# Up projection of a one-layer encoder: low halves of raw weight units from an accumulating DMA into buffers of their own, and thirteen pairs through seven products

## The chip, the core and the metric

The kernel runs on one core of one Trainium2 chip. The metric is the device time of one execution in microseconds (us). Three runs of the kernel before gave 1048.84, 1049.99 and 1050.54 us; their median, 1049.99 us, is the time that the change is measured against.

The engines are named as in the profile: PE is TensorE's matrix multiply and PEld its weight load, DVE is VectorE, ACT is ScalarE, POOL is GpSimd, SP is SyncE, whose queue issues most of the DMAs. All data is float32; fp32r is the rounded form of it that PE takes as an operand here.

## What is computed

One layer of an encoder: three token mixers with gated merging, cross-attention into a memory, and a gated MLP with a short causal convolution, over 512 tokens of 1024 channels. The change touches the MLP's first product alone:

```python
def conv_ffn(h, w_up, conv_w, conv_b, w_down):
    u = causal_dwconv(h @ w_up, conv_w) + conv_b      # w_up: 1024 x 5632
    a, b = jnp.split(u, 2, axis=-1)
    return (jax.nn.silu(a) * b) @ w_down              # w_down: 2816 x 1024
...
x = x + conv_ffn(rmsnorm(x, norm_ffn[l]), w_up[l], ffn_conv[l], ffn_conv_b[l], w_down[l])
```

## The kernel before

**Products in split form.** A float32 matrix is used as a high half (its fp32r rounding, made by an ACT copy) and a low half (the rest, made by a DVE subtraction of the high half). A product is then three passes on PE: high weight by high data, high weight by low data, low weight by high data. Weights come in units of 128x1024 float32 (512 KB). `load_unit` issues the load of a unit from the SP queue into one of three buffers `wraw`; `split_unit` (L182, L183) makes `whi` on ACT and `wlo` on DVE, each in one of two buffers (WB = 3, 2, 2).

**The up stage.** `h @ w_up` has 44 units. They are worked in 22 pairs m = 0..21: unit 2m gives channel block m of `a`, unit 2m+1 block m of `b`. `gated(m)` then does the convolution (ACT L1081, four DVE steps on L1083), the silu (ACT L1085) and the product `hid` (DVE L1087).

- A *plain* pair runs `up_product` twice. A unit is 24 matmuls of 512 columns: 16 with `whi` (L203, L204) and 8 with `wlo` (L206).
- A *seven* pair (m in SEVEN, `seven_products`) regards the two units as a 2x2 block matrix a11, a12, a21, a22 over halves of 512 channels and the tokens as two halves of 256, and needs seven half-size products in place of eight. Each (`half_product`) is 12 matmuls of 256 columns: 8 with a high half (L1021, L1024, L1025), 4 with a low half (L1027). It multiplies raw parts (a11, a12, a22) and sums of parts. DVE makes four sums (L1045, L1046, L1050, L1051, in `s12` and `s34`), ACT and DVE split both sum tiles (L1031, L1032: `sh`, `sl`), a1 whole and the half a22 (`whi`, `wlo`, also L1031, L1032). Five DVE steps of 256 columns (L1068 to L1073) put the products together.

SEVEN holds nine pairs: 7, 8, 9, 11, 13, 15, 16, 18, 20. The token sums that they multiply by (`token_forms`) are made behind pair 4 (FORMS).

**What sets the order.** The program is written pair after pair; a scheduler with a timeline of its own then places the instructions of each engine, and pools with a fixed number of buffers add waits: a new tile waits until all readers of the old one are done. Behind pair 18 come the splits of the first ten `hid` (`split_hidden`), behind the up stage those and the sums of the other twelve (`form_pair`), which go into `room` slots: the freed quads first, then eight tiles of pool `extra`. The pool `extra` is opened behind pair 4, where the pool `late` (x, spilled to DRAM by then) is closed. The down stage follows.

Of the kernel before, what the change touches and what calls it, by code (L numbers as in the profile page):

```python
# [78 lines left out]
def build(nc, tc, ctx, x_t, mem_t, w, cols_d, const_d, unit_d, out_t, dbg=None):  # L79
# [910 lines left out]
    def token_forms():  # L990


        pairs = []
        for name in ("14", "23"):
            pairs.append([hquad(f"t{name}{z}", F32R).rearrange("p a b -> p (a b)").rearrange("p (f k n) -> p f k n", f=2, k=4)
                          for z in "hl"])
        for k in range(4):
            e, o = values[k], values[k + 4]
            f = uwork(f"tf{k}")

            def two(t):
                return t.rearrange("p (f n) -> p f n", f=2)

            V.tensor_tensor(e[:, L], e[:, R], e[:, L], ALU.subtract)
            V.tensor_tensor(two(f), two(e), o[:, None, R].to_broadcast([P, 2, T // 2]), ALU.add)
            V.tensor_tensor(e[:, R], f[:, L], o[:, L], ALU.subtract)
# [6 lines left out]
    def half_product(ps, unit, x, behind=None):


        (wh, wl), (xh, xl) = unit, x
        with ExitStack() as order:
            if behind is not None:
                order.enter_context(tc.issue_after(behind.ins))
            new = behind is None  # L1020
            first = PE.matmul(ps, wh[:, block(0)], xh[:, 0], start=new, stop=False, skip_group_check=not new)  # L1021
            for i in range(4):
                if i:
                    PE.matmul(ps, wh[:, block(i)], xh[:, i], start=False, stop=False, skip_group_check=not new)  # L1024
                PE.matmul(ps, wh[:, block(i)], xl[:, i], start=False, stop=False, skip_group_check=not new)  # L1025
            for i in range(4):
                PE.matmul(ps, wl[:, block(i)], xh[:, i], start=False, stop=i == 3, skip_group_check=not new)  # L1027
        return first

    def split_blocks(src, hi, lo):  # L1030
        S.activation(hi, src, AF.Copy)  # L1031
        V.tensor_tensor(lo, src, hi.bitcast(F32), ALU.subtract)  # L1032
        return hi, lo

    def seven_products(m):


        u = UNITS["up"] + 2 * m
        a1, a2 = load_unit(u), load_unit(u + 1)
        a = [(t[:, :T], t[:, T:]) for t in (a1, a2)]  # L1040
        (a11, a12), (a21, a22) = a
        h1, l1 = wp.tile([P, 1024], F32R, tag="whi", name=f"whi{u}", bufs=WB[1]), wp.tile([P, 1024], F32R, tag="wlo", name=f"wlo{u}", bufs=WB[2])
# [1 line left out]
        s12, s34 = wsum(f"s12_{m}"), wsum(f"s34_{m}")
        V.tensor_tensor(s12[:, :T], a21, a22, ALU.subtract)  # L1045
        V.tensor_tensor(s12[:, T:], a11, s12[:, :T], ALU.subtract)  # L1046
        h12, l12 = split_blocks(s12, wsumh(f"sh12_{m}", F32R), wsuml(f"sl12_{m}", F32R))
        h2, l2 = wp.tile([P, 1024], F32R, tag="whi", name=f"whi{u + 1}", bufs=WB[1]), wp.tile([P, 1024], F32R, tag="wlo", name=f"wlo{u + 1}", bufs=WB[2])
# [1 line left out]
        V.tensor_tensor(s34[:, :T], a21, a11, ALU.subtract)  # L1050
        V.tensor_tensor(s34[:, T:], a12, s12[:, T:], ALU.subtract)  # L1051
        h34, l34 = split_blocks(s34, wsumh(f"sh34_{m}", F32R), wsuml(f"sl34_{m}", F32R))
        (b1h, b1l), (b2h, b2l) = halves
        px = dense_ps(f"px{m}")
        py = misc_ps(f"py{m}")
        pz = gdn_ps(f"pz{m}")
        first = half_product(px[:, L], (h1[:, :T], l1[:, :T]), (b1h[:, :, L], b1l[:, :, L]))
        half_product(px[:, R], (h12[:, :T], l12[:, :T]), t_forms[1], first)
        v = uwork(f"v{m}")
        S.activation(v, px, AF.Copy)  # L1060
        first_y = half_product(py[:, L], (h2[:, :T], l2[:, :T]), t_forms[4])
        half_product(pz[:, L], (h12[:, T:], l12[:, T:]), t_forms[2])
        half_product(px[:, L], (h1[:, T:], l1[:, T:]), (b2h[:, :, L], b2l[:, :, L]), first)
# [323 lines left out]
```

## Time and profile before

| | |
|---|---|
| median of three runs | 1049.99 us |
| the profiled execution, its own time | 1050.53 us |
| its span in the trace | 1048.8 us |
| up stage (first up matmul to first down matmul) | 692.38 to 929.11 us |
| PE busy, whole span | 1035.8 us, 99% |
| DVE, ACT, POOL busy, whole span | 756.6, 566.8, 28.7 us |
| granted TensorE clock | 1.00 |

Matmuls are pipelined: a row of 512 columns lasts 0.39 us, but the next one starts about 0.23 us behind it. The pace of PE is read from start to start, and so is that of DVE and ACT, whose rows overlap the next by some tenths of a microsecond or less. A busy share of PE near 1 says that it had an operand all the time.

### The profile page before, as it was taken

Reading aid. Unit: us, or ns where it says so; the run is one execution under the profiler, and the core shown is the slowest. Engines: PE = TensorE matmul, PEld = TensorE weight load, DVE = VectorE, ACT = ScalarE, POOL = GpSimd, SP = SyncE. Lnnn points to the kernel's source line nnn. Section 1 sums busy time; section 2 is a strip of 40 time slices with the busy share of each in tenths; the row PEclk is TensorE's granted clock in tenths of the full one; section 3 lists DMA queues with packets and bytes.
Section 4 is the critical chain, followed back from the end, with each engine's and each line's share of the span. In section 5 each row is a group of like instructions: output and inputs, shape, how many; then the busy total and the mean of one; then the engine's idle time right before and its main releaser. Section 6 shows DMA issues by size and latency. Waiting matters only on the chain.

```text
span 1048.8 us, 14151 instructions
## 1 busy us (share of the span) xinstructions
PE 1035.8 (99%) x5385; PEld 871.1 (83%) x5385; DVE 756.6 (72%) x1252; ACT 566.8 (54%) x936; POOL 28.7 (3%) x82
## 2 busy tenths in 40 slices
PE   9999999999999999999999999999999999999998
PEld 7787888778888888788888888778899999989997
DVE  5787668788455443446657757679898998899873
ACT  6376757646342644654545657655555645655331
POOL 0000000101010000000000000000000000000000
PEclk9999999999999999999999999999999999999999
DMA  6222121211211111222433333142322323233441
GB/s 234 88 93 101 64 78 61 71 61 62 80 61 61 61 41 61 81 81 90 164 108 121 123 105 115 41 161 83 118 100 93 107 96 109 81 105 117 146 156 61
DMA packets 29443, 100.61 MB, mean 96 GB/s; under 512 B 3392, under 2 KB 3648, under 8 KB 28864
## 3 DMA queue, kind: packets, MB, share of 16 engines
q1 hardware_dynamic: 29088, 99.45, 28.1%
q8 instruction: 42, 0.69, 0.3%
q10 hardware_dynamic: 288, 0.27, 0.1%
q14 instruction: 25, 0.20, 0.1%
HBM read 95.51 MB, written 4.19 MB: 95 GB/s over the span
## 4 chain that ended last, share of the span: by engine, by line
PE 94%; DVE 2%; ACT 1%; issue 1%; DMA 1%; SPq 0%; POOL 0%; ACTq 0%; DVEq 0%; POOLq 0%
PE dn L1186 8%; PE up L206 5%; PE up L204 4%; PE up L203 4%; PE g L203 4%; PE g L204 4%; PE g L206 4%; PE gk L374 2%; PE px L1027 2%; PE px L1025 2%; PE dz L1186 2%; PE dx L1186 2%; PE f L203 1%; PE s L206 1%; PE s L204 1%; PE f L206 1%
## 5 line engine op out<-in xcount | busy, mean ns | idle before, releaser
L182 ACT ACTIVATE whi<-wraw 128x1024 fp32r<-128x1024 f32 x133 | 140.7, 1058 | 169.3 <-PE g L204 38.7
L183 DVE TENSOR_TENSOR wlo<-wraw,whi 128x1024 fp32r<-128x1024 f32 x133 | 162.1, 1219 | 44.4 <-ACT whi L182 19.6
L203 PE MATMUL g<-hh,whi 128*128 128x512 f32 x192 | 77.5, 404 | 1.6 <-DVE gate L390 1.6
L204 PE MATMUL g<-hl,whi 128*128 128x512 f32 x192 | 75.7, 394 | 0.0
L204 PE MATMUL up<-xnl,whi 128*128 128x512 f32 x144 | 56.8, 394 | 0.0
L203 PE MATMUL up<-xnh,whi 128*128 128x512 f32 x144 | 56.8, 394 | 0.0
L206 PE MATMUL g<-hh,wlo 128*128 128x512 f32 x192 | 51.5, 401 | 0.0
L1186 PE MATMUL dn<-room,whi 128*128 128x256 f32 (+1 forms) x176 | 49.6, 333 | 0.0
L203 PEld LDWEIGHTS g<-hh,whi 128*128 128x128 f32 x192 | 36.1, 188 | 10.9 <-DVE gate L390 1.4
L206 PEld LDWEIGHTS g<-hh,wlo 128*128 128x128 f32 x192 | 35.8, 188 | 8.3 <-issue 0.5
L204 PEld LDWEIGHTS g<-hl,whi 128*128 128x128 f32 x192 | 36.2, 188 | 7.7
L390 DVE TENSOR_TENSOR gate<-g,r_x 128x512 f32<-128x512 f32 x24 | 16.4, 688 | 30.8 <-PE g L206 30.8
L1083 DVE SCALAR_TENSOR_TENSOR uc<-u,cols,uc 128x511 f32<-128x511 f32 (+1 forms) x52 | 37.0, 745 | 0.9 <-ACT uc L1081 0.9
L206 PE MATMUL up<-xnh,wlo 128*128 128x512 f32 x144 | 36.4, 395 | 0.0
L1186 PE MATMUL dn<-room,wlo 128*128 128x512 f32 (+1 forms) x128 | 34.1, 352 | 0.0
L1186 PEld LDWEIGHTS dn<-room,whi 128*128 128x128 f32 x176 | 29.8, 188 | 3.4
L203 PEld LDWEIGHTS up<-xnh,whi 128*128 128x128 f32 x144 | 27.1, 189 | 6.0
L204 PEld LDWEIGHTS up<-xnl,whi 128*128 128x128 f32 x144 | 27.1, 188 | 6.0
L206 PEld LDWEIGHTS up<-xnh,wlo 128*128 128x128 f32 x144 | 27.0, 188 | 6.2
L1186 PE MATMUL dn<-hidl,whi 128*128 128x512 f32 x80 | 31.6, 395 | 0.0
L1031 ACT ACTIVATE whi<-wraw 128x1024 fp32r<-128x1024 f32 (+1 forms) x18 | 15.2, 845 | 25.6 <-PE up L204 11.9
L1186 PEld LDWEIGHTS dn<-room,wlo 128*128 128x128 f32 x128 | 24.0, 188 | 3.5
(988 smaller groups left out, 2948.3 us busy)
## 6 DMA issues: line engine op xcount, KB each, us to landing
wraw<-w SPq DMA_DIRECT2D x166, 512.0 KB, 3.5
x<-x_t SPq DMA_DIRECT2D x8, 256.0 KB, 6.6
xr<-x_t SPq DMA_DIRECT2D x2, 1024.0 KB, 6.2
x_spill<-xr SPq DMA_DIRECT2D x2, 1024.0 KB, 4.3
x<-x_spill SPq DMA_DIRECT2D x8, 256.0 KB, 4.1
mem_sb<-mem_t SPq DMA_DIRECT2D x4, 256.0 KB, 4.1
wraw<-w SPq DMA_DIRECT2D x2, 256.0 KB, 4.1
inv<-unit ACTq DMA_DIRECT2D x1, 256.0 KB, 3.4
```

The costliest lines, as they stand in the source:

```text
L182: S.activation(hi, raw, AF.Copy)
L183: V.tensor_tensor(lo, raw, hi.bitcast(F32), ALU.subtract)
L203: PE.matmul(ps, hi[:, b], xh, start=first and i == 0, stop=False)
L204: PE.matmul(ps, hi[:, b], xl, start=False, stop=False)
L206: mm = PE.matmul(ps, lo[:, b], xh, start=False, stop=last and i == len(xs) - 1)
L374: pin(PE.matmul(first[h], a[:, c:c + P], b, start=k == 0 and a is hi and b is xh, stop=k == KC - 1 and b is xl))
L390: V.tensor_tensor(dst, ps, r_x, ALU.mult)
L1025: PE.matmul(ps, wh[:, block(i)], xl[:, i], start=False, stop=False, skip_group_check=not new)
L1027: PE.matmul(ps, wl[:, block(i)], xh[:, i], start=False, stop=i == 3, skip_group_check=not new)
L1031: S.activation(hi, src, AF.Copy)
L1083: V.scalar_tensor_tensor(c[:, s:], u[:, :T - s], col("ffn_conv", 3 * j + 2 - s), c[:, s:], ALU.mult, ALU.add)
L1186: mm = PE.matmul(ps[:, z], lhs, rhs, start=first is None, stop=last, skip_group_check=True)
```

## The change

It alters how the low halves of raw weight units are made in the up stage, which pairs run as seven products, and where one pool lies.

- `split_adding` makes a split without DVE: ACT writes minus the high half into a tile `alo`, POOL issues a DMA that adds the unit from DRAM to it (`accum_op=ALU.add`), and ACT makes `whi` as before. `alo` has four buffers of 128x1024 in a pool `ahead`, so two pairs' worth. It serves a1 (512 KB) and a22 (256 KB) of every seven pair, and both units of the plain pairs behind pair 4 (`ADD_PLAIN`; m > FORMS). That is 34 accumulating DMAs. The kernel before has no such DMA.
- SEVEN gains 10, 12, 14, 17, 19 and loses 15: thirteen pairs, with 7 to 14 in one run, 16 to 20 in another. The plain pairs behind pair 4 are 5, 6, 15 and 21.
- `ahead` takes the room of `extra` during the up stage; `extra` opens behind the loop.
- A seven pair puts its outputs together in place, without the tile `w`: again five DVE steps of 256 columns. The splits of the two sum tiles stay on ACT and DVE. Other edits only rename or merge helpers.

```diff
+AHEAD = 4
+ADD_A22 = True
+ADD_PLAIN = (0, 1)
-SEVEN = (7, 8, 9, 11, 13, 15, 16, 18, 20)
+SEVEN = (7, 8, 9, 10, 11, 12, 13, 14, 16, 17, 18, 19, 20)
...
+    ahead = tiles_of("ahead", "a", AHEAD, (1024,))
...
+    def split_adding(u, src, cols, name):
+
+        lo = ahead(f"alo{name}", F32R)[:, :cols.stop - cols.start]
+        hi = wp.tile([P, 1024], F32R, tag="whi", name=f"whi{name}", bufs=WB[1])[:, :cols.stop - cols.start]
+        S.activation(lo, src, AF.Copy, scale=-1.0)
+        G.dma_start(lo, w[u, :, cols], accum_op=ALU.add)
+        S.activation(hi, src, AF.Copy)
+        return hi, lo
...
+        h1, l1 = split_adding(u, a1, slice(0, 2 * T), f"{u}")
+        s1, s2, f12 = sums("12")
+        V.tensor_tensor(s1, a21, a22, ALU.subtract)
+        V.tensor_tensor(s2, a11, s1, ALU.subtract)
+        w5, w6 = f12()
+        if ADD_A22:
+            h2, l2 = split_adding(u + 1, a22, slice(T, 2 * T), f"{u + 1}")
...
-        split_blocks(a1, h1, l1)
...
-        split_blocks(a22, h2[:, :T], l2[:, :T])
...
-        mm3(ps, split_unit(UNITS["up"] + 2 * m + z), [block(k) for k in range(KC)], x, True, True)
+        u = UNITS["up"] + 2 * m + z
+        if z in ADD_PLAIN and m > FORMS:
+            unit = split_adding(u, load_unit(u), slice(0, 2 * T), f"{u}")
+        else:
+            unit = split_unit(u)
+        mm3(ps, unit, [block(k) for k in range(KC)], x, True, True)
...
             late.close()
-            open_pool("extra", ctx, side="right")
+            room = ExitStack()
+            open_pool("ahead", room, side="right")
         for _ in range(SPLITS.get(m, 0)):
             split_hidden()
+    room.close()
+    open_pool("extra", ctx, side="right")
```

The order in which the built program's instructions stand shows three places. A name ends in the number of its allocation. First, ACT in a seven pair, before: pair 11. `whi_7007` and `whi_7019` are the high halves of a1 and a22, `sh_11` those of the sums, `v` and `u` outputs of pair 9.

```order
L1031 ACTIVATE whi_7007<-wraw_7003 128x1024
L1031 ACTIVATE sh_11_7015<-s_11_7011 128x1024
L1070 ACTIVATE u_6911<-px_6821 128x256
L1031 ACTIVATE sh_11_7025<-s_11_7012 128x1024
L1031 ACTIVATE whi_7019<-wraw_7005 128x512
L1081 ACTIVATE uc_6919<-u_6911,cols 128x512
```

After: the same stretch for pair 10. `alo_7077` and `alo_7089` are the negated high halves of pair 11, one pair ahead of the others; POOL's DMA adds to each when it is written.

```order
L294 ACTIVATE whi_6942<-wraw_6937 128x1024
L292 ACTIVATE alo_7077<-wraw_7073 128x1024
L273 ACTIVATE sh_10_6949<-s_10_6946 128x1024
L1120 ACTIVATE uc_6790<-uc_6790 128x512
L294 ACTIVATE whi_6954<-wraw_6939 128x512
L292 ACTIVATE alo_7089<-wraw_7075 128x512
L273 ACTIVATE sh_10_6961<-s_10_6958 128x1024
L333 ACTIVATE u_6918<-px_6829 128x256
```

Two ACT copies per pair came in, each ahead of a sum's high half of the pair before it. Second, DVE in seven pairs 8 and 9, before:

```order
L1032 TENSOR_TENSOR sl_8_6673<-s_8_6668,sh_8_6672 128x1024
L1073 TENSOR_TENSOR u_6641<-px_6551,w_6640 128x256
L1032 TENSOR_TENSOR sl_8_6683<-s_8_6669,sh_8_6682 128x1024
L1045 TENSOR_TENSOR s_9_6803<-wraw_6797 128x512
L1032 TENSOR_TENSOR wlo_6800<-wraw_6795,whi_6799 128x1024
L1083 SCALAR_TENSOR_TENSOR uc_6649<-u_6641,cols,uc_6649 128x511
L1050 TENSOR_TENSOR s_9_6804<-wraw_6797,wraw_6795 128x512
```

After, the same place:

```order
L332 TENSOR_TENSOR u_6646<-px_6557,u_6646 128x256
L331 TENSOR_TENSOR u_6647<-u_6647,v_6584 128x256
L274 TENSOR_TENSOR sl_8_6690<-s_8_6686,sh_8_6689 128x1024
L1118 SCALAR_TENSOR_TENSOR uc_6654<-u_6646,cols,uc_6654 128x511
L314 TENSOR_TENSOR s_9_6822<-wraw_6803,wraw_6801 128x512
L315 TENSOR_TENSOR s_9_6822<-wraw_6801,s_9_6810 128x512
L1118 SCALAR_TENSOR_TENSOR uc_6658<-u_6647,cols,uc_6658 128x511
```

The subtraction `wlo` is gone; sums and splits of sums stay. Third, PE where the first low half of a seven pair is read, before (pair 7; in brackets what a row waits for):

```order
L1024 MATMUL pz_6553<-t23h,sh_7_6537 128x256
L1025 MATMUL pz_6553<-t23l,sh_7_6537 128x256
L1027 MATMUL px_6551<-xnh_5997,wlo_6530 128x256 [waits DVE_49]
L1027 MATMUL px_6551<-xnh_5997,wlo_6530 128x256 x3
L1021 MATMUL px_6551<-t14h,sh_7_6537 128x256
```

After (pair 8):

```order
L266 MATMUL px_6693<-xnh_5997,whi_6670 128x256
L267 MATMUL px_6693<-xnl_5998,whi_6670 128x256
L269 MATMUL px_6693<-xnh_5997,alo_6669 128x256 [waits DMASW6_49]
L269 MATMUL px_6693<-xnh_5997,alo_6669 128x256 x3
L263 MATMUL px_6693<-t14h,sh_8_6677 128x256 [waits Activation_49]
```

The low-half rows now wait for a DMA that POOL issued, where they waited for DVE. POOL has no other instruction behind pair 4. All engines' rows up to pair 4 stand as before.

## Rows read from the trace of the kernel before

**Rows 1.** The page: span and busy time of each engine, and the first line of the chain that ended last, by engine.

```profile
span 1048.8 us, 14151 instructions
...
PE 1035.8 (99%) x5385; PEld 871.1 (83%) x5385; DVE 756.6 (72%) x1252; ACT 566.8 (54%) x936; POOL 28.7 (3%) x82
...
PE 94%; DVE 2%; ACT 1%; issue 1%; DMA 1%; SPq 0%; POOL 0%; ACTq 0%; DVEq 0%; POOLq 0%
```

**Rows 2.** Busy time of each engine in stretches of the up stage and the start of the down stage: from and to, length, busy time of PE, PEld, DVE, ACT and POOL (with counts), granted clock, DMA share (mean of the 16 engines), GB/s.

```profile
768.00:800.00 32.00, 32.00 (x241) 30.64 (x240) 30.34 (x45) 17.27 (x23) 0.00 (x0) 1.00 0.35 118
800.00:840.00 40.00, 40.00 (x259) 36.34 (x258) 35.75 (x55) 22.55 (x30) 0.00 (x0) 1.00 0.31 103
840.00:880.00 40.00, 40.00 (x274) 37.09 (x274) 35.83 (x55) 20.72 (x28) 0.00 (x0) 1.00 0.32 106
880.00:920.00 40.00, 40.00 (x255) 36.22 (x254) 34.88 (x52) 25.25 (x38) 0.00 (x0) 1.00 0.27 93
```

**Rows 3.** What PE and its weight load waited for from 690 us to the end of the span: us in total, times, longest. It is the whole answer for both.

```profile
PE up L204 <- DVE xfl L196: 0.7, 2, 0.5
...
PEld up L204 <- DVE xfl L196: 1.6, 2, 1.0
```

**Rows 4.** PE in order of time (start, us, line, operation, count): the first matmul of the up stage, the first of one plain unit, that unit's low-half rows and the first matmul of the next unit, and the first of the down stage.

```profile
692.38 0.39 PE L203 MATMUL up<-xfh,whi 128*128 128x512 f32 x1
...
716.36 0.39 PE L203 MATMUL up<-xfh,whi 128*128 128x512 f32 x1
...
720.08 2.02 PE L206 MATMUL up<-xfh,wlo 128*128 128x512 f32 x8
721.93 0.40 PE L203 MATMUL up<-xfh,whi 128*128 128x512 f32 x1
...
929.11 0.40 PE L1186 MATMUL dn<-room,whi 128*128 128x512 f32 x1
```

**Rows 5.** The same view in seven pairs: the first matmul of one half product of 12, its low-half rows and the first matmul behind it; and the same of another.

```profile
777.84 0.28 PE L1021 MATMUL py<-t23h,sh 128*128 128x256 f32 x1
...
778.80 0.64 PE L1027 MATMUL py<-t23h,sl 128*128 128x256 f32 x4
779.28 0.28 PE L1021 MATMUL px<-xnh,whi 128*128 128x256 f32 x1
...
781.53 0.28 PE L1021 MATMUL px<-xnh,sh 128*128 128x256 f32 x1
...
782.49 0.64 PE L1027 MATMUL px<-xnh,sl 128*128 128x256 f32 x4
782.97 0.28 PE L1025 MATMUL px<-xnl,whi 128*128 128x256 f32 x1
```

**Rows 6.** DVE in order of time, a stretch without idle time in a seven pair.

```profile
783.47 0.42 DVE L1072 SCALAR_TENSOR_TENSOR u<-py,w 128x256 f32<-128x256 f32 x1
783.80 1.22 DVE L1032 TENSOR_TENSOR sl<-s,sh 128x1024 fp32r<-128x1024 f32 x1
784.93 0.42 DVE L1073 TENSOR_TENSOR u<-px,w 128x256 f32<-128x256 f32 x1
785.27 1.22 DVE L1032 TENSOR_TENSOR sl<-s,sh 128x1024 fp32r<-128x1024 f32 x1
786.40 0.68 DVE L1045 TENSOR_TENSOR s<-wraw 128x512 f32<-128x512 f32 x1
787.00 1.22 DVE L1032 TENSOR_TENSOR wlo<-wraw,whi 128x1024 fp32r<-128x1024 f32 x1
788.14 0.74 DVE L1083 SCALAR_TENSOR_TENSOR uc<-u,cols,uc 128x511 f32<-128x511 f32 x1
788.80 0.69 DVE L1050 TENSOR_TENSOR s<-wraw,wraw 128x512 f32<-128x512 f32 x1
789.40 0.75 DVE L1083 SCALAR_TENSOR_TENSOR uc<-u,cols,uc 128x511 f32<-128x511 f32 x1
```

**Rows 7.** ACT in order of time: a half-size copy, the silu, the `v` copy and the `u` copy of seven pairs, and a stretch without idle time.

```profile
885.11 0.63 ACT L1031 ACTIVATE whi<-wraw 128x512 fp32r<-128x512 f32 x1 [1.43 <-PE up L204]
...
887.87 0.63 ACT L1085 ACTIVATE uc<-uc 128x512 f32<-128x512 f32 x1
889.85 0.60 ACT L1060 ACTIVATE v<-px 128x512 f32<-128x512 f32 x1 [1.34 <-PE px L1027]
...
896.99 0.39 ACT L1070 ACTIVATE u<-px 128x256 f32<-128x256 f32 x1 [2.05 <-PE px L1027]
...
900.57 0.80 ACT L1081 ACTIVATE uc<-u,cols 128x512 f32<-128x512 f32 x1
901.27 1.04 ACT L1031 ACTIVATE sh<-s 128x1024 fp32r<-128x1024 f32 x1
902.22 1.04 ACT L1031 ACTIVATE whi<-wraw 128x1024 fp32r<-128x1024 f32 x1
```

**Rows 8.** The page's DMA queue that carries all loads (packets, MB, time of its packets as a share of the 16 engines' span) and three of its issues (count, KB each, median us from issue to landing).

```profile
q1 hardware_dynamic: 29088, 99.45, 28.1%
...
wraw<-w SPq DMA_DIRECT2D x166, 512.0 KB, 3.5
...
xr<-x_t SPq DMA_DIRECT2D x2, 1024.0 KB, 6.2
x_spill<-xr SPq DMA_DIRECT2D x2, 1024.0 KB, 4.3
```

More of the change, by code (lines that the diff above doesn't have):

```diff
@@ L239, in project_heads, with two, half_product @@
                 yield 2 * g + q, ps
+    LEFT, RIGHT = slice(0, T // 2), slice(T // 2, T)
+    def two(t):
+        return t.rearrange("p (f n) -> p f n", f=2)
+    def half_product(ps, unit, xs, behind=None):
+        wh, wl = unit
+        with ExitStack() as order:
+            if behind is not None:
+                order.enter_context(tc.issue_after(behind.ins))
+            new = behind is None
+            first = PE.matmul(ps, wh[:, block(0)], xs[0][0], start=new, stop=False, skip_group_check=not new)
+            for i, (xh, xl) in enumerate(xs):
+                if i:
+                    PE.matmul(ps, wh[:, block(i)], xh, start=False, stop=False, skip_group_check=not new)
+                PE.matmul(ps, wh[:, block(i)], xl, start=False, stop=False, skip_group_check=not new)
+            for i, (xh, _) in enumerate(xs):
+                PE.matmul(ps, wl[:, block(i)], xh, start=False, stop=i == 3, skip_group_check=not new)
+        return first
@@ new lines, in split_blocks, with halves_of, sums_of_tokens @@
+    def split_blocks(src, hi, lo):
+        S.activation(hi, src, AF.Copy)
+        V.tensor_tensor(lo, src, hi.bitcast(F32), ALU.subtract)
+        return hi, lo
+    def halves_of(xs, h, z):
+        return [(hi[:, z], lo[:, z]) for hi, lo in xs[4 * h:4 * h + 4]]
+    def sums_of_tokens(e, o, f):
+        V.tensor_tensor(e[:, LEFT], e[:, RIGHT], e[:, LEFT], ALU.subtract)
+        V.tensor_tensor(two(f), two(e), o[:, None, RIGHT].to_broadcast([P, 2, T // 2]), ALU.add)
+        V.tensor_tensor(e[:, RIGHT], f[:, LEFT], o[:, LEFT], ALU.subtract)
@@ L996, in token_forms @@
                           for z in "hl"])
+        forms = {1: [], 2: [], 3: [], 4: []}
         for k in range(4):
[L998 to L1006, printed above, removed]
@@ L1007, in token_forms @@
-            for t, (hi, lo) in zip((e, f), pairs):
+            e, f = values[k], uwork(f"tf{k}")
+            sums_of_tokens(e, values[k + 4], f)
+            for t, (hi, lo), (p, q) in zip((e, f), pairs, ((1, 4), (2, 3))):
                 S.activation(hi[:, :, k], two(t), AF.Copy)
                 V.tensor_tensor(lo[:, :, k], two(t), hi[:, :, k].bitcast(F32), ALU.subtract)
-        (h14, l14), (h23, l23) = pairs
-        return {1: (h14[:, 0], l14[:, 0]), 4: (h14[:, 1], l14[:, 1]), 2: (h23[:, 0], l23[:, 0]), 3: (h23[:, 1], l23[:, 1])}
@@ L1013, in half_product @@
[L1013 to L1042, printed above, removed]
-        split_blocks(a1, h1, l1)
[L1044 to L1048, printed above, removed]
-        split_blocks(a22, h2[:, :T], l2[:, :T])
[L1050 to L1063, printed above, removed]
-        half_product(py[:, R], (h34[:, :T], l34[:, :T]), t_forms[3], first_y)
-        half_product(px[:, R], (h34[:, T:], l34[:, T:]), (b2h[:, :, R], b2l[:, :, R]), first)
-        w = uwork(f"w{m}")
-        u0, u1 = uwork(f"u{m}"), uwork(f"u{m + NF}")
-        V.tensor_tensor(w[:, L], pz[:, L], v[:, L], ALU.add)
-        V.tensor_tensor(w[:, R], py[:, R], w[:, L], ALU.add)
-        S.activation(u0[:, L], px[:, L], AF.Copy)
-        V.tensor_tensor(u1[:, R], w[:, R], v[:, R], ALU.add)
-        V.scalar_tensor_tensor(u1[:, L], py[:, L], -1.0, w[:, R], ALU.mult, ALU.add)
-        V.tensor_tensor(u0[:, R], px[:, R], w[:, L], ALU.add)
-        return u0, u1
@@ new lines, in token_forms, with seven_up, sums, split_sums @@
+                for z, i in enumerate((p, q)):
+                    forms[i].append((hi[:, z, k], lo[:, z, k]))
+        return forms
+    def seven_up(m):
+        def sums(which):
+            t = wsum(f"s{which}_{m}")
+            def split_sums():
+                h, l = split_blocks(t, wsumh(f"sh{which}_{m}", F32R), wsuml(f"sl{which}_{m}", F32R))
+                return [(h[:, z], l[:, z]) for z in (slice(0, T), slice(T, 2 * T))]
+            return t[:, :T], t[:, T:], split_sums
+        return seven(UNITS["up"] + 2 * m, str(m), xn, t_forms, sums, lambda: (uwork(f"u{m}"), uwork(f"u{m + NF}")), uwork)
```

75 lines of the change are left out of this document (50 added, 25 removed).

## The prediction

> **What bounds the kernel now.** I read the page first: PE is busy 99% of the span and 94% of the chain that ended last is PE [rows 1]. The second view is the table of stretches: from 768 to 920 us PE is busy in every microsecond, the granted clock is 1.00, DVE is busy for 30.34 of 32 us, then 35 of 40, ACT for about half, POOL not at all [rows 2]. The third is the list of waits: behind 690 us PE and its weight load wait for others 0.7 and 1.6 us in all, at the start of the up stage [rows 3]. So PE is the bound and never starves. There is no stall to remove: the time falls only by work taken from PE, and only while every operand still comes in time. DVE is the engine next to it, and stands between PE and more seven pairs.
>
> **The gain on PE.** A plain unit takes from 716.36 to 721.93, 5.57 us for 24 matmuls [rows 4], a pair 11.14. A half product of 12 takes 1.44 us (777.84 to 779.28, and 781.53 to 782.97) [rows 5], seven of them 10.08. Check against the whole stage: 692.38 to 929.11 is 236.7 us [rows 4]; 13 x 11.14 + 9 x 10.08 = 235.5, and with the 1.2 us that is left, waits of [rows 3], it closes. A pair that changes sides therefore gives 1.06 us of PE; four more seven pairs (13 for 9) give **4.2 us**. The down stage keeps its matmuls.
>
> **DVE.** From start to start in [rows 6] a step of 1024 columns takes 1.13 us (783.80 to 784.93), of 512 0.60 (786.40 to 787.00), the convolution's 0.66 (788.14 to 788.80), of 256 0.34. A seven pair before: three splits of 1024 (3.39), one of 512 and four sums (3.00), five outputs (1.70), four convolution steps (2.64), one product (0.60): 11.33 us, more than PE's 10.08. A plain pair: 2.26 + 2.64 + 0.60 = 5.50. Before, seven pairs were therefore mixed with plain ones. The eight in a row that the change makes (7 to 14) would need 90.6 us of DVE for 80.6 of PE if they were split the old way. The change takes one split of 1024 and one of 512 away: 9.60 us per seven pair, 76.8 for the run, 95% of PE's time; a plain pair behind pair 4 falls to 3.24. Pairs 7 to 21 together: before 9 x 11.33 + 6 x 5.50 = 135, after 13 x 9.60 + 2 x 3.24 = 131. DVE stays under PE, though hardly in the run. Its relief by itself costs and gives nothing, as PE hides it; it is what allows the 4.2.
>
> **ACT.** Each seven pair gains a copy of 1024 (0.95 from start to start, 901.27 to 902.22) and one of 512 (0.63) [rows 7]. Its sum: four of 1024 (3.80), two of 512 (1.26), `v` 0.60, `u` 0.39, two scalings at 0.70, the silu 0.63: 8.1 of 10.08 us, 80%. Hidden by PE; if ACT comes late, the sums' high halves, which stand behind `alo` on it, make PE wait. A waiting `alo` holds up exactly those: it waits for its raw unit and for a free buffer.
>
> **POOL and the accumulating DMA.** POOL's queue holds nothing else in this stage, so each of the 34 issues waits for its own ACT copy alone; the first also for the spill of x, whose two issues precede nearly all of the up stage's loads, and pair 5 is only due 55 us into it (5 x 11.14). What the trace does not show is how long such a DMA takes. From below: a plain load of the same 512 KB lands in 3.5 us. From above: a read of 512 KB and behind it one with twice the bytes, 3.5 + 6.2 = 9.7 us [rows 8]. It must read two operands of 512 KB, so the nearest row is the 1024 KB load, 6.2 us; I take that.
>
> The Trainium skill, "Collectives: The Full Stack", section "The bandwidth ceiling: the fold count and why AG ≠ RS ≠ AR", says that an addition inside the DMA engine costs no cycles of its own but needs two source reads, which halves the rate (62 against 32 GB/s there). By it the accumulating DMA is an estimated twice a plain one; no run here shows it yet, and it lies on the value that the rows gave.
>
> How long may it take? In the built program's order `alo` of pair 13 stands on ACT ahead of `sh` of pair 12, which PE needs at the second product of pair 12. From there to the first use of pair 13's low half PE has 56 matmuls of 256 columns at 0.12 us (1.44 / 12), 6.7 us, and the `sh` copy takes 0.95: at least 7.6 us of lead, if ACT is only just in time. Some seven of the 512 KB DMAs have a lead near that, most others 10.5 us (80 matmuls) or more. The 256 KB ones have 6.4 us or more, for half the bytes. At 6.2 us all land in time. Nothing is then on PE's path.
>
> **DMA engines.** The 99.45 MB of loads take 28.1% of the engines' span [rows 8], 295 us for all 16, so 1.55 us per 512 KB. A seven pair loads two units (3.1 us) and adds 768 KB: at twice the price of a load 4.7 us, together 7.8 of 10.08. The share rises from 0.31-0.35 [rows 2] to about 0.8. The Trainium skill, "DMA: Bandwidth & Descriptors", section "Issuing engines are not separate DMA queues", speaks against the change here: DMAs of every issuing engine share the same 16 engines. By it the raw loads land later than 3.5 us; the share above already counts them together. The three raw buffers bear some of it: held from the `alo` copy to the `whi` copy, one pair at most, two units need 2 x (3.5 + 10.1) = 27 us of 3 x 10.1 = 30.
>
> **Sum.** The profiled execution took 1050.53 us (span 1048.8, 1.7 around it), 0.54 above the median of the runs. 1050.5 - 4.2 = 1046.3 against it; against the median 1050.0, 1045.8. I forecast **1045.8**, 0.4% faster.
>
> **Rivals.**
> 1. *DVE or ACT becomes the bound in the run of seven pairs* and eats the gain. For it: 95% and 80% load, in queues that wait for each other and for PE in turn. Against: from 768 to 800 us, three old seven pairs, DVE reached 95% and PE missed nothing [rows 2]. If DVE gets through only the 89% of its time that it was busy from 800 to 880, the run takes 76.8 / 0.89 = 86.3 in place of 80.6: 5.7 us lost, 1051.5; at 95% (30.34 / 32) 80.9, 0.3 lost. Middle about 1049.
> 2. *The accumulating DMA lands late* (the slower side). Place: PE's first low-half matmul of each product, which holds up all of PE, since its queue goes in order. It decides from 7.6 us on. At the upper bound of 9.7 us seven of the DMAs miss by 2 us: 14 us, 1060, less where ACT ran ahead. The gain is gone at about 8.2 us. A worse form: the DMA engines fill up. 3.1 + 2.33 k reaches 10.08 at k = 3, k being the price of an added byte in plain ones; at k = 4 each seven pair takes 2.3 us more and each plain one 4.4 us, 1093. For it: no row shows such a DMA; POOL makes its descriptors, unlike SP's. Against: k = 2 by the bytes moved.
> 3. *The change does not do what it says*, the pairs give no time: 1050. It needs a half product of 1.59 us, where two in [rows 5] agree on 1.44; unlikely.
>
> **How the numbers follow.** Forecast (PE stays fed, 1044.5 to 1047.5) 0.59; rival 1 0.18 (1046.5 to 1051.5); rival 2 0.20 (two thirds below 1060); rival 3 0.03. What this kernel's measurement can tell from no change is 0.2%, 2.1 us: faster is below 1047.9, slower above 1052.1. Faster: 0.59 + 0.04 of rival 1 = 0.63. Same: 0.14 + 0.03 = 0.17. Slower: 0.20. The range goes from 1044.5 (the sum, less the 1.2 us by which runs lay under the median) to 1055, which takes in rival 1 and the milder part of rival 2; about 0.17 is left out above it, 0.02 below.
>
> **What the profile after would show.** If right: the up stage ends at about 925 us, PE waits in it as little as before, DVE's `wlo` subtractions are gone behind pair 4, accumulating DMAs land in 5 to 7 us, DMA share 0.7 to 0.8, DVE near 95% from pair 7 to 14. If rival 1: PE waits for `sh`, `sl` or `whi` in pairs 8 to 14, with DVE at 100%. If rival 2: PE waits for DMA at the `alo` rows. The prediction is wrong if such a DMA takes over 8 us, or if a wait for the raw units spreads through ACT's queue.

## The result, and the profile after

The changed kernel takes **1044.27 us** (median of four, 1043.75 to 1044.74) against 1050.03 us of the kernel before in the same runs: ratio 0.9947, 95% interval [0.9929, 0.9964]. It is faster, as forecast, and 0.2 us below the low end of the range. The profiled execution took 1044.74 us. Its page, for [rows 1, 8]: span, busy time, the queue of the accumulating DMAs, and the issues (count, KB each, us to landing).

```profile
span 1043.0 us, 14582 instructions
...
PE 1029.4 (99%) x5529; PEld 873.1 (84%) x5529; DVE 748.8 (72%) x1262; ACT 602.8 (58%) x986; POOL 58.1 (6%) x116
...
q1 hardware_dynamic: 29088, 99.45, 28.3%
q0 software_dynamic: 4896, 14.42, 8.4%
...
wraw<-w SPq DMA_DIRECT2D x166, 512.0 KB, 3.5
alo<-w POOLq DMA_DIRECT2D x21, 512.0 KB, 6.4
alo<-w POOLq DMA_DIRECT2D x13, 256.0 KB, 5.8
```

PE is still the bound. The stretches of [rows 2], after:

```profile
768.00:800.00 32.00, 32.00 (x258) 31.37 (x258) 27.02 (x44) 23.32 (x33) 6.03 (x7) 1.00 0.78 177
800.00:840.00 40.00, 40.00 (x339) 40.00 (x338) 36.84 (x61) 30.93 (x43) 6.90 (x8) 1.00 0.76 182
840.00:880.00 40.00, 40.00 (x293) 37.86 (x293) 34.40 (x56) 30.90 (x42) 6.90 (x8) 1.00 0.83 192
880.00:920.00 40.00, 40.00 (x306) 38.50 (x305) 37.70 (x65) 32.69 (x50) 4.31 (x5) 1.00 0.69 160
```

PE is full in all four, the DMA share has risen from about 0.3 to 0.8, ACT from about half to 73 to 82%, and DVE, with more pairs to serve, is busy 84 to 94%. What PE and its weight load waited for behind 690 us is the whole of [rows 3] again, and nothing else:

```profile
PE up L213 <- DVE xfl L205: 0.7, 2, 0.5
```

```profile
PEld up L213 <- DVE xfl L205: 1.6, 2, 1.0
```

The up stage (first `up` matmul to first `dn` matmul) runs from 691.28 to 923.27, 231.99 us in place of 236.73: 4.74 less. The down stage is as long as before. The other 1.1 us between these two traces lie before the up stage, in instructions that the change does not touch. They go back to the first products of the program. PE in order of time there, in the kernel before, and then in a second profile of the changed kernel (a2):

```profile
6.25 2.07 PE L374 MATMUL gk<-hh,ghi 128*128 128x512 f32 x4 [0.68 <-ACT hh L366]
8.12 1.91 PE L374 MATMUL gk<-hh,glo 128*128 128x512 f32 x4
9.83 1.36 PE L374 MATMUL gk<-hl,ghi 128*128 128x512 f32 x4
11.03 1.10 PE L374 MATMUL gk<-hh,ghi 128*128 128x512 f32 x4
```

```profile
6.13 1.20 PE L469 MATMUL gk<-hh,ghi 128*128 128x512 f32 x4 [1.00 <-ACT hh L461]
7.16 1.10 PE L469 MATMUL gk<-hh,glo 128*128 128x512 f32 x4
8.10 1.08 PE L469 MATMUL gk<-hl,ghi 128*128 128x512 f32 x4
9.02 1.10 PE L469 MATMUL gk<-hh,ghi 128*128 128x512 f32 x4
```

Four matmuls go from start to start in 1.87 us in the first and 1.03 in the second. This is TensorE's clock. Each trace holds a record of the granted clock; it begins, at the upper of the two levels (2.4 GHz), at 10.40 us in the first profile and at 4.46 us in the second. Ahead of that point matmuls of 512 columns start 0.43 us apart, behind it 0.23. The pace of 0.43 is that of the lower level (1.2 GHz): in e4, where the record shows that level from 791.3 to 798.2 us, matmuls of 256 columns start 0.21 us apart, and 0.12 outside it.

Such a **late beginning** puts the products behind it back by 1.7 to 2.1 us. Between the profiles before and after it was 1.7 us; 1.1 of them are left at the up stage, since on the way there one wait of PE, for an ACT copy of a weight, was 0.5 us longer after than before (0.8 against 0.3). Is it of the kernel or of the execution? The experiments had to say.

### The profile page after: what moved, and what is told of

Read it like the earlier page. It is cut to its first block, busy times and chain, and to the rows that moved or that the text cites. A ratio compares the mean times of both kernels' runs of the same rounds, so it can differ in the third digit from the quotient of the medians.

```text
span 1043.0 us, 14582 instructions
## 1 busy us (share of the span) xinstructions
PE 1029.4 (99%) x5529; PEld 873.1 (84%) x5529; DVE 748.8 (72%) x1262; ACT 602.8 (58%) x986; POOL 58.1 (6%) x116
## 3 DMA queue, kind: packets, MB, share of 16 engines
q1 hardware_dynamic: 29088, 99.45, 28.3%
q0 software_dynamic: 4896, 14.42, 8.4%
## 4 chain that ended last, share of the span: by engine, by line
PE 94%; DVE 2%; ACT 1%; DMA 1%; issue 1%; SPq 0%; POOL 0%; ACTq 0%; DVEq 0%; POOLq 0%
PE dn L1221 8%; PE g L212 4%; PE g L213 4%; PE g L215 4%; PE up L215 3%; PE up L213 3%; PE up L212 3%; PE px L267 2%; PE px L269 2%; PE gk L469 2%; PE px L266 2%; PE dz L1221 2%; PE dx L1221 2%; PE f L212 1%; PE s L213 1%; PE s L215 1%
## 5 line engine op out<-in xcount | busy, mean ns | idle before, releaser
L186 ACT ACTIVATE whi<-wraw 128x1024 fp32r<-128x1024 f32 x117 | 123.8, 1058 | 150.4 <-PE g L213 38.7
L187 DVE TENSOR_TENSOR wlo<-wraw,whi 128x1024 fp32r<-128x1024 f32 x117 | 142.7, 1220 | 42.7 <-ACT whi L186 21.4
L293 POOL DMA_DIRECT2D alo<-w x34 | 29.5, 866 | 422.2 <-ACT alo L292 419.8
L294 ACT ACTIVATE whi<-wraw 128x1024 fp32r<-128x1024 f32 (+1 forms) x34 | 30.3, 892 | 15.9 <-PE py L267 8.8
L292 ACT ACTIVATE alo<-wraw 128x1024 fp32r<-128x1024 f32 (+1 forms) x34 | 30.2, 887 | 13.1 <-DMA wraw<-w 12.1
L274 DVE TENSOR_TENSOR sl<-s,sh 128x1024 fp32r<-128x1024 f32 x26 | 31.8, 1223 | 5.2 <-ACT sh L273 5.1
L212 PE MATMUL up<-xnh,whi 128*128 128x512 f32 x80 | 31.6, 395 | 0.0
L213 PE MATMUL up<-xnl,whi 128*128 128x512 f32 x80 | 31.6, 395 | 0.0
L273 ACT ACTIVATE sh<-s 128x1024 fp32r<-128x1024 f32 x26 | 27.3, 1051 | 5.6 <-PE px L267 3.2
L1116 ACT ACTIVATE uc<-u,cols 128x512 f32<-128x512 f32 x34 | 26.7, 809 | 4.5 <-DVE u L1191 3.6
```

The source lines that it names most:

```text
L186: S.activation(hi, raw, AF.Copy)
L187: V.tensor_tensor(lo, raw, hi.bitcast(F32), ALU.subtract)
L212: PE.matmul(ps, hi[:, b], xh, start=first and i == 0, stop=False)
L213: PE.matmul(ps, hi[:, b], xl, start=False, stop=False)
L292: S.activation(lo, src, AF.Copy, scale=-1.0)
L293: G.dma_start(lo, w[u, :, cols], accum_op=ALU.add)
```

## The experiments

The theory: four pairs give what a pair gives, nothing else changed, and the late beginning belongs to the execution. Rivals: the adding DMA gives or costs something by itself; DVE had room for more pairs anyway; the changed program itself begins earlier.

**a1 and a2: both kernels unchanged.**

> The kernel before, unchanged, against itself. Question: how much of the 5.6 us between the medians is variation between executions, and does the first stretch of the program (where the profile of after was 1.1 us ahead, in instructions that are the same in both) vary. Theory 1 (the 1.1 us come from one profiled execution and not from the kernel): ratio 1.000 with an interval that may reach 0.1%, the up stage (first up product to first down product) again 236.7 +- 0.1 us, and its beginning anywhere from 691.2 to 692.5 us. Theory 2 (the changed kernel's first stretch is itself faster): the up stage begins at 692.3 to 692.5 us again.

> The changed kernel, unchanged, in more rounds. Theory 1 (four more pairs at 1.14 us each, nothing else): up stage 232.0 us, 4.6 to 4.8 us shorter than that of before, and the time 4.6 us below before, ratio 0.9955 to 0.9957. Theory 2 (something besides the pairs, worth 1 us): ratio 0.9946 again.

a1: 1049.02 us, ratio 0.9998 [0.9989, 1.0007], up stage 237.03, beginning at 691.0: early, as theory 1 has it, though both figures lie 0.2 us outside those of theory 1. a2: 1044.12 us, ratio 0.9949 [0.9936, 0.9961], up stage 232.37; the interval holds the ratios of both theories, and the stage, 4.66 us shorter than a1's, speaks for theory 1. Over all runs, 90 executions of the kernel before fall into 60 from 1048.04 to 1049.74 (median 1048.92) and 30 from 1049.99 to 1051.21 (median 1050.55), though only 0.25 us lie between the groups. Of the first three, on whose median the forecast rested, two were of the upper group, the profiled one among them. The stages differ by 236.9 - 232.2 = 4.7 us in the mean of the two profiles each.

**f0: the changed kernel a third time.**

> The changed kernel a third time. Question: do its executions ever begin late, as 12 of 31 of the kernel before did in one batch (times from 1050.0 up, against 1048.3 to 1049.7 for the others). Theory 1 (a late beginning has nothing to do with the change, nine early ones were chance): with each further execution a chance of about 0.3 to 0.4 of a time of 1045.5 to 1046.5, so one to three of the new ones. Theory 2 (the changed program begins early always): all of them 1043.7 to 1044.8.

1044.33 us, ratio 0.9951 [0.9937, 0.9965], with two of five at 1045.45 and 1045.59. The profiled one is of these, and shows the late beginning in the changed kernel (its clock record begins at 10.72 us):

```profile
6.16 2.08 PE L469 MATMUL gk<-hh,ghi 128*128 128x512 f32 x4 [0.59 <-ACT hh L461]
8.04 1.91 PE L469 MATMUL gk<-hh,glo 128*128 128x512 f32 x4
```

Its up stage is 231.99 us all the same. Theory 1: the late beginning is the execution's. Median of all 14 executions of the changed kernel 1044.24, of all 90 of the kernel before 1049.07.

**e1: the adding DMA without the four pairs.** **e6: eleven pairs.**

```diff
-SEVEN = (7, 8, 9, 10, 11, 12, 13, 14, 16, 17, 18, 19, 20)
+SEVEN = (7, 8, 9, 11, 13, 15, 16, 18, 20)          # e1
+SEVEN = (7, 8, 9, 10, 11, 12, 13, 15, 16, 18, 20)  # e6
```

> The accumulating DMA alone: the changed kernel with the nine pairs of before in seven products. TensorE then has the work of before. Theory 1 (the adding DMA only makes room on VectorE, and by itself is worth nothing): up stage 236.7 us, ratio 1.000 within 0.1%. Theory 2 (VectorE or its share of SBUF held TensorE up somewhere, so the relief is worth time by itself): up stage shorter by over 0.5 us, ratio below 0.9993. Theory 3 (the doubled DMA work costs something that the gain of the pairs hides): ratio above 1.0007.

> Eleven pairs through seven products (7 to 13, 15, 16, 18, 20), the dose between nine and thirteen, everything else as in the changed kernel. Theory 1 (each pair gives the same, no threshold): up stage 234.4 to 234.5 us, half way between 236.7 and 232.2, time 1046.2 to 1046.5 us where the changed kernel has 1044.1. Theory 2 (the gain of the pairs is partly eaten by something that sets in with the long runs): less than half of the gain is missing, 1045 us or under.

e1: 1048.54 us, ratio 0.9993 [0.9985, 1.0002], up stage 236.74, where the kernel before had 236.73 and 237.03. e1 holds every edit of the change but the pairs. Relieving DVE gives nothing by itself, and the adding DMA's extra work costs nothing. e6: 1046.38 us, ratio 0.9974 [0.9965, 0.9984], up stage 234.38, half way. The gain goes by the number of pairs. The size of a pair is read from start to start of the same matmul of two pairs; in the changed kernel, two seven pairs in a row:

```profile
782.50 0.28 PE L263 MATMUL px<-t14h,sh 128*128 128x256 f32 x1
```

```profile
792.48 0.28 PE L263 MATMUL px<-t14h,sh 128*128 128x256 f32 x1
```

9.98 us a seven pair. In e1, over a seven pair and a plain one:

```profile
791.52 0.28 PE L263 MATMUL px<-t14h,sh 128*128 128x256 f32 x1
```

```profile
812.69 0.28 PE L263 MATMUL px<-t14h,sh 128*128 128x256 f32 x1
```

21.17, so a plain pair takes 11.19, and the exchange is worth **1.21 us**. Read by itself, from its first matmul to the first one behind it, a plain pair of e1 takes 11.17; the other 0.02 lie where it borders on a seven pair:

```profile
800.09 0.39 PE L212 MATMUL up<-xnh,whi 128*128 128x512 f32 x1
...
811.26 0.28 PE L263 MATMUL px<-xnh,whi 128*128 128x256 f32 x1
```

By the stages, a pair is worth 1.17 (a1 against a2) to 1.19 us (before against after).

**e2: the thirteen pairs without the adding DMA.** **e5: DVE splits a22 alone again.**

```diff
-ADD_A22 = True
-ADD_PLAIN = (0, 1)
+ADD_A22 = False   # e2 and e5
+ADD_PLAIN = ()    # e2
...
-        h1, l1 = split_adding(u, a1, slice(0, 2 * T), f"{u}")
+        h1, l1 = (wp.tile([P, 1024], F32R, tag=t, name=f"{t}{u}", bufs=b) for t, b in (("whi", WB[1]), ("wlo", WB[2])))   # e2
+        split_blocks(a1, h1, l1)   # e2
```

> The pairs alone: thirteen pairs in seven products, but all low halves split by VectorE as before, no accumulating DMA. Theory 1 (VectorE needs 11.3 us for a pair of which TensorE needs 10.0): in the run of eight pairs VectorE falls behind by 8 x 1.3 = 10 us, less what its buffers hold (one pair at most), so TensorE waits 3 to 10 us there, and up to 6 us more in the run of five; the time is 1047 to 1056 us, the gain of 4.6 us mostly or wholly lost. Theory 2 (VectorE keeps pace from the slack of the plain pairs, and the adding DMA was not needed): TensorE waits under 0.5 us, the time is that of the changed kernel, 1044 to 1046 us.

> The changed kernel with the 256 KB accumulating DMA left out: the low half of the fourth block of each pair is split by VectorE again, the 512 KB ones stay. VectorE then needs 10.2 us for a pair of which TensorE needs 10.0. Theory 1 (VectorE binds where its work per pair is over TensorE's, less one pair of cushion): 8 x 0.2 = 1.6 us behind in the run of eight, all within the cushion, so the time of the changed kernel within 0.5 us, 1044.1 to 1044.6. Theory 2 (no cushion, the excess of 13 pairs is paid in full, with the hand-overs): 2 to 5 us over it, 1046 to 1049.

e2: 1055.40 us, ratio 1.0058 [1.0046, 1.0071]. DVE (the third busy time) has no idle time left, and PE (the first) starves:

```profile
800.00:840.00 40.00, 37.71 (x305) 36.44 (x304) 40.00 (x64) 24.16 (x33) 0.00 (x0) 1.00 0.29 93
840.00:880.00 40.00, 38.75 (x273) 35.84 (x273) 39.50 (x62) 23.20 (x32) 0.00 (x0) 1.00 0.29 94
```

So the pairs need the DMA: without it they cost 6.1 us against the kernel before (1049.32 in that batch), with it, in a2, they save 5.2. e5 missed both expectations: 1055.92 us, ratio 1.0058 [1.0037, 1.0079], as slow as e2, for 0.60 us of DVE work a pair. DVE is not full: busy 36.41 of 40 us from 800 to 840. PE waits, and then DVE's:

```profile
PE px L263 <- ACT sh L273: 4.2, 3, 2.1
PE px L263 <- ACT v L321: 2.2, 3, 1.4
PE px L263 <- ACT whi L294: 1.7, 1, 1.7
PE py L269 <- DVE wlo L274: 1.7, 4, 0.7
```

```profile
DVE uc L1118 <- ACT uc L1116: 11.4, 7, 4.4
DVE sl L274 <- ACT sh L273: 6.1, 5, 1.5
...
DVE s L305 <- DMA wraw<-w: 4.1, 4, 2.0
```

PE waits for ACT, DVE for ACT and for a raw unit: time lost in hand-overs between queues, not in an engine without rest. PE's waits in this list, 9.8 us, are most of the 13.2 by which the up stage is longer than the changed kernel's (245.4 us).

**e4: two buffers for the adding DMA, not four.** **e9: a copy in the place of the addition.**

```diff
-AHEAD = 4
+AHEAD = 2                                       # e4
...
-        G.dma_start(lo, w[u, :, cols], accum_op=ALU.add)
+        G.dma_start(lo, w[u, :, cols])          # e9
```

> The changed kernel with two buffers for the adding DMA, not four: a pair's first buffer is then free only when the product before the last two of the pair ahead has been read. Theory 1 (landing takes 6.4 us after the issue, as in the profile, and the lead decides): the copy (1.1 us), the issue (0.9 us) and the landing need some 8 us, TensorE can cover 2.9 us of two products and 0.9 us of the next one's first matmuls, so it waits some 4 us for the adding DMA in each of the pairs that follow a pair: 40 to 60 us over the changed kernel, 1085 to 1105. Theory 2 (the landing time is mostly queueing behind other transfers and shrinks when fewer are ahead): half of that or less, 1045 to 1065.

> The changed kernel with a plain copy in the place of the accumulating one, on the same queue, of the same bytes (so the low halves hold whole weights, and the subtraction is left out). Theory 1 (accumulating costs the second time): the queue's share of DMA time falls from 8.4% to 4 to 5%, that is from 3.2 to 1.6 us of sixteen engines per 512 KB, landing from 6.0 to 6.4 us to about 3.5 to 4, DMA share between 770 and 920 us from 0.76 to 0.83 down to about 0.5. Theory 2 (it is the price of this queue, not of adding): share and landing as before. The time stays at 1044 us either way, since TensorE waited for none of these transfers.

e4: 1092.42 us, ratio 1.0401 [1.0358, 1.0444], the time of theory 1, though by another sum: PE waits for the adding DMA once in each of the thirteen pairs, but for 2.2 us and not some 4:

```profile
PE px L269 <- DMA alo<-w: 29.2, 13, 3.1
PE up L215 <- DMA alo<-w: 1.9, 3, 1.1
PE py L269 <- DMA alo<-w: 1.8, 3, 0.8
```

That is 33 of some 50 us. Much of the rest is TensorE's clock (the eighth field): the granted clock was 0.87 to 0.96 in the stretches from 768 to 960 us, 1.00 in those of the changed kernel. The trace has 30.7 us there at the lower level; at 0.21 us a matmul in place of 0.12 that is an estimated 13 us at most.

```profile
768.00:800.00 32.00, 24.99 (x168) 23.44 (x167) 18.93 (x29) 15.54 (x21) 4.28 (x5) 0.89 0.53 130
800.00:840.00 40.00, 34.83 (x274) 34.03 (x274) 29.41 (x48) 25.19 (x35) 5.18 (x6) 0.96 0.60 145
```

So "one pair ahead" is what makes the adding DMA free. e9: 1044.75 us in its one execution, with the queue's work and the landings cut:

```profile
q0 software_dynamic: 4896, 14.42, 4.6%
...
alo<-w POOLq DMA_DIRECT2D x21, 512.0 KB, 4.7
alo<-w POOLq DMA_DIRECT2D x13, 256.0 KB, 4.2
```

8.4% of 1043.0 us for 14.42 MB is 3.19 us of the 16 engines per 512 KB; the copy takes 4.6%, 1.74; a load of SP's queue 1.56 (28.3% for 99.45 MB). The addition nearly doubles the work, theory 1; the DMA share from 770 to 920 us falls from 0.77 to 0.56. But the copy lands in 4.7 us, not the 3.5 to 4 expected, still 1.2 us behind a load of SP's: of the 2.9 us by which the adding DMA is later, 1.7 go with the addition and 1.2 with the rest of this path.

**e3 and e7: fifteen pairs. e8: e5 with more room. e10: seventeen. f1, f2, f3, g1: fourteen. e11: thirteen.** Could more be had? e3 and g1 change SEVEN alone (15 and 21 added; 6 added). The others also load a pair's second unit into the idle `wlo` buffers, which makes five raw buffers of three (e8: into `ahead`).

```diff
-        a1, a2 = load_unit(u), load_unit(u + 1)
+        a1 = load_unit(u)
+        a2 = wp.tile([P, 1024], F32, tag="wlo", name=f"wraw{u + 1}", bufs=WB[2])
+        nc.sync.dma_start(a2, w[u + 1])
```

> Fifteen pairs through seven products: pairs 15 and 21 as well, so that all from 7 to 21 are. Theory 1 (a pair is worth 1.1 to 1.2 us wherever VectorE, ScalarE and the adding DMA keep up, and they do): 2.3 us below the changed kernel, 1041.8 us, no new waits of TensorE. Theory 2 (VectorE's slack is used up: it was busy 94% between 880 and 920 us in the changed kernel, and two more pairs put some 10 us of work on it, 146 of 150 us from 770 to 920): TensorE waits for VectorE for 2 to 8 us in the last pairs or at the start of the down stage, and the time is that of the changed kernel or up to 4 us over it.

> Fifteen pairs through seven products, as in e3, with one edit: the second weight unit of each such pair is loaded into the two buffers that held low halves before and stand idle in this stage, so five raw buffers stand in the place of three. No engine's work changes. Theory 1 (what held e3 up is the ring load - sums - buffer free - next load with only three raw buffers, not the sum of VectorE's work): TensorE's waits go, up stage 229.6 to 229.8 us (two more pairs at 1.2 us under the changed kernel's 232.0 to 232.4), time 1041.6 to 1042.2. Theory 2 (VectorE's total work binds, 97% of the stretch): the waits of e3 stay, 1050 us or more.

> The kernel of e5 (fourth block's low half by VectorE, 256 KB adding DMA left out) with one edit: the second unit of each pair is loaded into the buffers of the adding DMA, of which this kernel uses one of two per pair, so raw units have more room. Theory 1 (e5 lost its 11.8 us to the ring of three raw buffers, which that split held longer, while VectorE was under 92% busy): time of the changed kernel again, 1044.0 to 1045.0. Theory 2 (VectorE, at 10.2 us of work against 9.98 of TensorE per pair, binds): TensorE waits stay, 1050 us or more. In between, 1045 to 1050, both share.

> All pairs from 5 to 21 through seven products, seventeen, with the five raw buffers of e7. Theory 1 (each pair is worth 1.2 us as long as nothing waits): 1039.3 to 1040.0 us, up stage 227.2 to 227.5 us. Theory 2 (VectorE, which also forms the token sums and splits of this stage between 735 and 770 us and was busy 88% there, falls behind at the start of the run): TensorE waits 1 to 6 us between 720 and 770 us and the gain over e7 is gone, 1041 to 1047.

> Fourteen pairs through seven products, pair 6 added to the thirteen, and five raw buffers as in e7. Pair 6 lies where VectorE is 88% busy with the token sums and their splits. Theory 1 (room before the run, the limit lies at its end): one pair's 1.2 us below the changed kernel, 1042.9. Theory 2 (VectorE carries its arrears from there through the run of nine): TensorE waits 1 to 4 us, 1044 to 1047.

> Fourteen pairs, pair 15 added, so that 7 to 20 run without a plain pair between them, with five raw buffers. Theory 1 (the limit is the work due before the down stage; 15 lies far ahead of it, and VectorE has until 21 to make it up): 1042.9, no waits. Theory 2 (the plain pair 15 is what lets VectorE catch up): the wait of 1.4 us near 872 us that e7 and e10 show stays, and VectorE enters the last pairs late: 1044 to 1048.

> Fourteen pairs, pair 21 added, the last of the stage, with five raw buffers. Theory 1 (the limit is an unbroken run): 1042.9. Theory 2 (the down stage's first splits by VectorE are due right behind pair 21, and a pair of 9.6 us of VectorE's work in the place of a plain one pushes them back): TensorE waits at the start of the down stage, 4 to 6 us in all, as in e7 from 922 to 972 us, and the time is 1046 to 1049.

> Fourteen pairs with pair 6 added, as in f1, but with the three raw buffers of the changed kernel. Theory 1 (the wait of 1.38 us in f1 comes of the order that five raw buffers bring, and VectorE has room for pair 6): no such wait, 1.2 us below the changed kernel, 1042.9 to 1043.1. Theory 2 (VectorE has no room for pair 6, or three raw buffers no longer do): TensorE waits 1.5 us or more, 1044.3 or over.

> The thirteen pairs of the changed kernel with the five raw buffers of e7, no other edit. Theory 1 (five raw buffers bring an order in which ScalarE's copy of a product stands behind a weight copy that waits for TensorE): a wait of some 1.4 us for that copy once or twice, 1045.5 to 1047. Theory 2 (the order is harmless, the waits of e7, f1 and f2 come from the added pairs): 1044.1 to 1044.3.

| | pairs added | raw buffers | us (median) | ratio to before |
|---|---|---|---|---|
| e11 | none | 5 | 1046.20 | 0.9966 [0.9952, 0.9979] |
| g1 | 6 | 3 | 1050.06 | 1.0006 [0.9996, 1.0016] |
| f1 | 6 | 5 | 1044.46 | 0.9952 [0.9937, 0.9966] |
| f2 | 15 | 5 | 1046.77 | 0.9974 [0.9964, 0.9984] |
| f3 | 21 | 5 | 1045.56 | 0.9966 [0.9954, 0.9978] |
| e3 | 15, 21 | 3 | 1055.33 | 1.0052 [1.0035, 1.0069] |
| e7 | 15, 21 | 5 | 1049.65 | 1.0009 [1.0000, 1.0019] |
| e10 | 5, 6, 15, 21 | 5 | 1060.17 | 1.0108 [1.0093, 1.0123] |
| e8 | none, a22 by DVE | 3, and 2 of `ahead` | 1054.07 | 1.0049 [1.0032, 1.0066] |

None beats the changed kernel: above thirteen pairs each one more costs what it gives, or more. e3 and e10 took more than either expectation had. Three limits stand close together.

*The raw buffers.* The same pairs take 5.6 and 5.7 us less with five (f1 against g1, e7 against e3); theory 1 of e7 holds for half of e3's loss. Part of that is the clock: granted 0.96 in g1 from 768 to 800 us and in e3 from 840 to 880, 1.00 in f1 and e7. In e11 they neither give nor cost: up stage 232.04 us and no wait of PE but the old one. Its median lies in the range of theory 1 all the same, because its profiled execution, and by their times two others of the four, began late, and 0.3 to 0.4 us more than in a2 and f0 lie outside the span of the trace; the fourth took 1044.39. In e8 more room gave back only 1.9 us of the 11.8 that e5 lost against a2; but there the raw units shared the adding DMA's buffers, and PE waited 4.6 us for that DMA, so it does not settle what e5 lost its time to.

*A ring through ACT's queue.* In f1 PE lost 1.38 us in one place, where it needed ACT's copy `v`; then ACT ahead of it:

```profile
812.06 0.39 PE L263 MATMUL px<-xnh,whi 128*128 128x256 f32 x1 [1.38 <-ACT v L323]
```

```profile
809.76 1.06 ACT L273 ACTIVATE sh<-s 128x1024 fp32r<-128x1024 f32 x1 [1.39 <-PE px L267]
810.73 0.80 ACT L1118 ACTIVATE uc<-u,cols 128x512 f32<-128x512 f32 x1
811.43 0.57 ACT L323 ACTIVATE v<-px 128x512 f32<-128x512 f32 x1
```

`v` stands behind a copy `sh` that had itself waited 1.39 us for PE. That one wait takes the 1.2 us that pair 6 gives and a little more. f2 and e7 show the same wait of 1.38 us; f2 another of 1.33 for a `whi`. e11, without a 14th pair, shows none: theory 2 there.

*The work due before the down stage.* In f3, with pair 21, PE waits in the down stage for ACT's `whi` and `sdh` (0.9 and 0.4 us). In e7, from 920 to 960 us, DVE (the third busy time) is at 96%, against 92% in the changed kernel:

```profile
920.00:960.00 40.00, 38.59 (x206) 32.42 (x205) 38.47 (x66) 25.93 (x42) 0.00 (x0) 1.00 0.27 92
```

Up and down stage of e7 together take 6.0 us more than the changed kernel's, though two pairs have become cheaper: theory 2 of f3 in kind, though smaller than it said (f3 lost some 2.7 us against its 1042.9, not 4 to 6). That DVE's load is what sets it off is not shown: f2 has DVE at 96% in the same stretch, and PE is full there. In e10 the pair put first also waits 6.3 us for ACT's high half of a token sum, and the granted clock is 0.90 from 720 to 770 us.

## Why the prediction came out as it did

The direction, the bound and the mechanism were right: PE was full before and after, and four pairs' worth of its work is what left. The time lay 1.5 us below the forecast. The step that failed is the sum: two of its terms were mis-sized, what a pair gives and the base that it is taken from, and together they make up the miss.

- **The pair: mis-sized.** "A pair that changes sides gives 1.06 us": it gives 1.21 by the pace, 1.17 to 1.19 by the stages. A half product is 9.98 / 7 = 1.43 us, not the 1.44 of the two rows in [rows 5], and a plain pair 11.17 to 11.19, not twice the 5.57 of one unit [rows 4]. A difference of 0.014 us, seven times over, and one of up to 0.05 made 12% of a small difference. The check against the whole stage could not see it, since one error was up and the other down: with the new figures 13 x 11.19 + 9 x 9.98 = 235.3 of 236.7, as close as the 235.5 of the forecast. Nor does the check close as it says: of the 1.2 us left over, PE's waits in [rows 3] are 0.7. Four pairs are 4.84 us by the pace and 4.7 by the stages, not 4.2: 0.5 to 0.6 us of the miss. Shown by e1, e6, a2 and the stages.
- **The base: the median of three runs.** "Against the median 1050.0": two of those three, the profiled one among them, were of the upper third. Over 90 executions the kernel before has a median of 1049.07: 0.9 us of the miss. This part is chance: of the 5.8 us between the two medians of the first runs, 4.8 are the kernel's. 1045.8 - 0.6 - 0.9 = 1044.3; the median of the 14 executions of the changed kernel is 1044.24. Shown by a1, a2 and f0. The low end of the range allowed for the spread of the base alone (1045.8 - 1.2, which is 1044.6 and not 1044.5), and so had no room for a pair worth more.
- **DVE: right, with less margin than it looks.** 95% was forecast for the run of eight pairs; it was busy 84 and 92% in the two stretches there. That its relief is worth nothing alone (e1) and carries the gain (e2) held. Rival 1 did not come up at thirteen pairs, but by e5 0.60 us of DVE's work a pair more is enough for a loss. The forecast priced it by DVE's load; but e5 lost its time in hand-overs between ACT, DVE and PE, with DVE busy 83 to 91%, and f1 in one between ACT and PE, with DVE at 95%. (In rival 1, 76.8 us at 95% are 81.0, not 80.9.)
- **ACT: right.** 80% forecast, 77% in the stretches from 800 to 880.
- **The adding DMA and its lead: right.** 6.2 us forecast, 6.4 measured; PE never waited for it. Rival 2 did not come up with four buffers, and e4 shows that it is the lead that keeps it away: at two buffers it costs 48 us. The rise of the DMA share to 0.8 was right too (0.69 to 0.83). The Trainium skill, "Collectives: The Full Stack", section "The bandwidth ceiling: the fold count and why AG ≠ RS ≠ AR", has the addition in a collective halve the rate, because two operands are read; e9 agrees for this DMA: 3.19 against 1.74 us per 512 KB on the same queue, 1.83 times.
- **Raw buffers: right for thirteen.** 27 of 30 us were called bearable; they were, and the raw loads landed hardly later from 770 to 915 us (3.6 us, 3.5 before). Above thirteen pairs, two buffers more are worth 5.6 us.
- **The end of the up stage**: 925 forecast, 923.3 found; 1.1 us of the difference lie before the up stage, in the two profiled executions.

Open: why e5 loses 11.8 us for 0.60 us of DVE work a pair. The queues' order in the built program differs from the changed kernel's as well, and e8 did not part the two. Open also why TensorE's clock rises late in some executions.

## What to carry to other kernels

Where a gain is a small difference of two large paces, read each over many repetitions in a row (six pairs, not one half product), because a few hundredths of a microsecond per step decide the sum; and ask of a median of three which executions are in it. An operation that was moved off a busy engine pays only through the work that the engine can now take on, and costs nothing only as long as its lead is longer than its landing: here four buffers against two were 48 us. When a kernel has been filled up to its neighbours' limits, the next step of the same kind (a 14th pair) can cost more than it gives, with none of PE's neighbours at 100%.

## What the runs showed that was not expected

- The program begins with TensorE at its lower clock level, and the rise comes early or late. The clock record begins at 9.8 to 10.7 us in five of the 20 profiles (before, f0, e2, e7, e11) and at 4.4 to 6.3 us in the other fifteen, and in each the matmuls of 512 columns change from 0.43 to 0.23 us there. PE's first nine matmuls run from 1.4 to about 5.5 us, then it waits for ACT until about 6; in the fifteen the clock rises ahead of that wait, in it or about its end, in the five only when the next products are under way. By their times, 30 of 90 executions of the kernel before and 2 of 14 of the changed one begin late. A view by stretches does not show it, as it counts time ahead of the record as full clock (last but two of the fields, the kernel before):

```profile
8.00:11.00 3.00, 3.00 (x9) 2.32 (x9) 1.36 (x3) 1.75 (x4) 0.00 (x0) 1.00 1.03 405
```

- A wait in a busy stage can cost more than its length, by the clock that falls behind it: granted 0.87 to 0.96 in e4 with waits of up to 3.1 us, and 0.96 in g1 behind four waits of 0.2 to 0.7 us from 761 to 768 us. But e5, with single waits of up to 2.1 us, kept 1.00 in the up stage. Which waits cost clock, these rows do not settle.
- An issue of the adding DMA kept POOL 0.87 us, of the plain copy on the same queue 0.53.
